# Feed-forward operands moved to starts of their own within 256 bytes, stage by stage

## The chip, the core and the metric

The kernel runs on one core of a Trainium2 chip. The metric is the time of one execution on the device in microseconds (us). Three runs of the kernel before gave 983.25, 983.36 and 985.91; the median is 983.36 us.

The engines are named as in the profile: PE is the matrix engine (PEld its weight loads), DVE the vector engine, ACT the scalar engine, POOL the general one, SP the queue that issues nearly all transfers. SBUF is the on-chip memory of 128 partitions; a "place" below is the byte at which a tile starts in every partition, taken modulo 256. PSUM is the memory that PE writes its sums to.

## The reference

One batch of 256 tokens with 1024 features goes through two layers in float32. What matters here is the feed-forward block, which stands four times in the program, before and after the mixer of each layer:

```python
def swiglu(x, w_gate, w_up, w_down):
    return (jax.nn.silu(x @ w_gate) * (x @ w_up)) @ w_down
...
h = h + 0.5 * swiglu(rms_norm(h, ffn1_norm_g[layer]), ffn1_w_gate[layer],
                     ffn1_w_up[layer], ffn1_w_down[layer])
```

`w_gate` and `w_up` are 1024 x 2816, `w_down` is 2816 x 1024. Between the blocks stand a convolution mixer with memory attention (layer 0), a shared key and value projection, and a block attention mixer with memory attention (layer 1), each with an output projection.

## The kernel before, in words

Activations lie transposed: features over partitions, the 256 tokens along the free dimension. The kernel wants float32 accuracy from products in the faster float32r type, so every operand is split in two: a high part `h` (the value rounded to float32r) and a low part `l` (the rest). A product is made of three of the four partial products, `h*h`, `h*l` and `l*h`.

**Operands.** A streamed operand of a feed-forward stage is one tile `y[P, k, 2, 256]` (or `hs[P, 22, 2, 256]` for the hidden values), in which for each of the `k` blocks of 128 features the high and low parts stand side by side. Weights come from memory in chunks of 2048 columns (`raw`, 1 MB, three buffers, one transfer each on SP's queue). `half_hi` takes half a chunk: ACT copies it into `wh` (line 185: the rounding is the high part) and DVE subtracts `wh` from `raw` into `wl` (line 189). `wh` and `wl` have four buffers of 1024 columns each, that is eight weight tiles of 128 x 128.

**Passes.** One weight load and the stream behind it is called a pass here. For a pair of sums in one PSUM bank, `mm_run` makes from a half chunk eight passes with `wh`, over 512 columns (`y` high and low), and eight passes with `wl`, over 256 columns (`y` high alone). All of them go through line 152. `next_turn` flips which kind goes first, so that two runs of the same kind stand next to each other: `wl` x8, `wh` x8, `wh` x8, `wl` x8 and so on. The last of the eight output tiles of a down projection goes through `mm3` instead, three passes of 256 columns per weight tile.

**Stages.** `ffn` is called four times, with the names a, b, c and d. Each call is two stages: gate and up (22 steps of a gate group and an up group, tiles such as `bg`, `bu`), and down (eight output tiles of 22 weight tiles each, such as `bo`). That makes eight stages with eight streamed operands: `y0`, `ahs`, `oay`, `bhs`, `by1`, `chs`, `oby`, `dhs`. Per call there are 176 wide passes and 176 narrow ones for gate, as many for up, and for down 154 wide and 220 narrow (176 with `wl`, 44 with `wh` in the last output tile). Over the program that is 2024 wide and 2288 narrow passes.

**Order.** A tile framework orders the instructions of each engine from the program's dependencies with its own timing model; tile pools set where each tile lies. The pools are laid one behind another in SBUF: `yp` (streamed operands), `op` (`wh`), `hp` (hidden values), `sp`, `lp` (`wl`), `cp`, `wp` (`raw`), `tp`, `ps` in PSUM. The pool `sp` holds a single small tile `mhalf` of `STEP` = 16 values, 64 bytes, ahead of `lp`. In the built program every streamed operand and every `wh` starts at place 128, and every `wl` at place 192. The same buffers serve the mixers' projections (`ca`, `cg`, `mq`, `bq`, `kv`, `mkv`, `oao`, `obo`). In some of these (`kv`, `bq`, `mq`, `mkv`) the activations are the loaded operand and the weights are streamed.

Of the kernel before, what the change touches and what calls it, by code (L numbers as in the profile page):

```python
# [9 lines left out]
F32 = mybir.dt.float32  # L10
F32R = mybir.dt.float32r
# [6 lines left out]
P = 128  # L18
DM = 1024
KD = DM // P  # L20
SEQ = 256
NT = SEQ // P
DFF = 2816
KF = DFF // P
# [14 lines left out]
HC = 1024  # L39
# [11 lines left out]
MEM_AT = 9  # L51
FIRST_CAT = 3
TURN_AT = 2
STEP = 16
Q_AT = 6
CNR_AT = 4

# [27 lines left out]
def tile_kernel(ctx: ExitStack, tc: tile.TileContext, w, xT, memT, pos, vec, hg, const, out):  # L85
    nc = tc.nc
    yp = ctx.enter_context(tc.tile_pool(name="yp", bufs=2))
    op = ctx.enter_context(tc.tile_pool(name="op", bufs=4))
    hp_ = ctx.enter_context(tc.tile_pool(name="hp", bufs=1))
    sp = ctx.enter_context(tc.tile_pool(name="sp", bufs=1))  # L90
    lp = ctx.enter_context(tc.tile_pool(name="lp", bufs=4))
    cp = ctx.enter_context(tc.tile_pool(name="cp", bufs=1))
    wp = ctx.enter_context(tc.tile_pool(name="wp", bufs=3))
    tp = ctx.enter_context(tc.tile_pool(name="tp", bufs=2))
# [30 lines left out]
    nc.vector.memset(onel, 1.0 / PW)  # L125
    onem = cp.tile([P, P], F32, name="onem")
    nc.vector.memset(onem, 1.0 / PW)
    mhalf = sp.tile([P, STEP], F32, name="mhalf")
    nc.vector.memset(mhalf, -0.5)


    state = {"flip": False, "chunk": 0, "half": 0, "raw": None, "order": "", "last": {}}

    def behind(i, other):
        tc.add_manual_dep(i.ins, other.ins.name,
# [37 lines left out]
    def half_hi():  # L173
        n, h = state["chunk"], state["half"]
        if h == 0:
            state["raw"] = load_chunk(n)
        raw = state["raw"][:, h * HC:(h + 1) * HC]
        wh = op.tile([P, HC], F32R, name=f"wh{n}_{h}", tag="wh", bufs=4)
        wl = lp.tile([P, HC], F32R, name=f"wl{n}_{h}", tag="wl", bufs=4)
        state["chunk"], state["half"] = (n, 1) if h == 0 else (n + 1, 0)  # L180
        q = HC // 2 if n < 2 else HC
        parts = [slice(c, c + q) for c in range(0, HC, q)]

        def hi(s):
            state["act"] = nc.scalar.activation(wh[:, s], raw[:, s], AF.Copy)  # L185
            return state["act"]

        def lo(s):
            state["dve"] = nc.vector.tensor_tensor(wl[:, s], raw[:, s], wh[:, s].bitcast(F32), op=ALU.subtract)  # L189
            return state["dve"]  # L190
        return wh, wl, parts, hi, lo
# [8 lines left out]
    def tiles_of(n_half):  # L200
        for n in range(n_half):
            wh, wl = half_chunk()
            for i in range(8):
                yield wh[:, i * P:(i + 1) * P], wl[:, i * P:(i + 1) * P]
# [47 lines left out]
        return ps.tile([P, 512], F32, name=name, tag=tag, bufs=bufs)  # L252


    def y_tiles(name):
        return yp.tile([P, KD, 2, SEQ], F32R, name=name, tag="y")

    def y_both(name):
        whole = yp.tile([P, KD, 2, SEQ], F32, name=name + "w", tag="y")
        return y_tiles(name), whole[:, :, 0]  # L260

    def scaled_split(y, src, k, g, on_dve=False):
# [62 lines left out]
    def new_acc(name):  # L325
        return tp.tile([P, SEQ], F32, name=name, tag="acc")

    def ffn(name, y, acc, nexts, store=False, both=False, hook=None, after=None, hook_down=None):

        hs = hp_.tile([P, KF, 2, SEQ], F32R, name=name + "hs", tag="hs")  # L330
        rb, first = None, acc is None
        for j in range(KF):
            if hook and j > 1:
                with tc.issue_after(state["act"].ins), tc.issue_after(state["dve"].ins), \
                        tc.issue_after(state["sync"].ins):
                    hook(j)
            if first and j == 0:

                four = [psum(f"{name}{'gu'[i % 2]}{i // 2}") for i in range(4)]
                it = tiles_of(4)  # L340
                for k in range(KD):
                    wts = [next(it) for _ in four]
                    for o, wt in zip(four, wts):
                        mm_passes(mm_run([(o, wt, k)], y)[:1], k == 0, False)
                    for o, wt in zip(four, wts):
                        mm_passes(mm_run([(o, wt, k)], y)[1:], False, k == KD - 1)
                acc = new_acc(name + "acc0")
                nc.scalar.dma_start(cst, const)

                sq = cp.tile([P, KD, SEQ], F32, name="sq0", tag="kv")  # L350
                for k in range(KD):
                    nc.scalar.activation(sq[:, k], x[:, k], AF.Square)
                n = KD
                while n > 1:
                    n //= 2
                    add = nc.vector.tensor_tensor(acc if n == 1 else sq[:, :n].rearrange("p k s -> p (k s)"),
                                                  sq[:, :n].rearrange("p k s -> p (k s)"),
                                                  sq[:, n:2 * n].rearrange("p k s -> p (k s)"), op=ALU.add)
                    if n == KD // 2:
                        behind(add, state["dve"])  # L360
            if first and j < 2:
                pg, pu = four[2 * j:2 * j + 2]
            else:

                at = ("sc", 2) if first and j == 2 else ()
                pg, pu = psum(f"{name}g{j}", *at), psum(f"{name}u{j}", *at)
                if j == 0:

                    wts = [list(tiles_of(1)) for _ in range(2)]
                    for ks in (range(KD - 1), (KD - 1,)):  # L370
                        runs = [mm_run([(o, wt[k], k) for k in ks], y, i == 1)
                                for i, (o, wt) in enumerate(zip((pg, pu), wts))]
                        for run in runs:
                            mm_passes(run, ks[0] == 0, ks[0] > 0)
                else:
                    mm_group2(pg, y)
                    mm_group2(pu, y)
            if rb is None:
                _, rb = norm_stats(name + "n", acc)
            g = both_halves(f"{name}gs{j}", pg, "g")  # L380
            nc.vector.tensor_tensor(g, g, rb, op=ALU.mult)
            s = tp.tile([P, SEQ], F32, name=f"{name}s{j}", tag="s")
            state["func"] = nc.scalar.activation(s, g, AF.Silu)
            h = both_halves(f"{name}h{j}", pu, "h")
            nc.vector.tensor_tensor(h, h, s, op=ALU.mult)
            nc.scalar.activation(hs[:, j, 0], h, AF.Copy)
            nc.vector.tensor_tensor(hs[:, j, 1], h, hs[:, j, 0].bitcast(F32), op=ALU.subtract)
        if after:
            tables(after)
        ys = [(y_both if both else y_tiles)(f"{name}y{i}") for i in range(len(nexts))]  # L390
        acc = new_acc(name + "acc")
        it = tiles_of(KD * KF // 8)
        for m in range(KD):
            po = psum(f"{name}o{m}")
            if hook_down:
                with tc.issue_after(state["act"].ins):
                    hook_down(m)

            both_sums = m < KD - 1
            if both_sums:  # L400
                lead = -m * KF % 8
                cuts = [0] * (lead > 0) + list(range(lead, KF, 8)) + [KF]
                for a, b in zip(cuts, cuts[1:]):
                    jobs = [(po, next(it), k) for k in range(a, b)]
                    mm_passes(mm_run(jobs, hs, next_turn()), a == 0, b == KF)
            else:
                for k in range(KF):
                    mm3(po[:, :SEQ], next(it), hs, k, k == 0, k == KF - 1)
            if both_sums:
                d = both_halves(f"{name}d{m}", po, "g")  # L410
                nc.vector.scalar_tensor_tensor(d, d, 0.5, rb, op0=ALU.mult, op1=ALU.mult)
            else:
                d = tp.tile([P, SEQ], F32, name=f"{name}d{m}", tag="g")
                nc.vector.scalar_tensor_tensor(d, po[:, :SEQ], 0.5, rb, op0=ALU.mult, op1=ALU.mult)
            nc.vector.tensor_tensor(x[:, m], d, x[:, m], op=ALU.add)
            if store:
                nc.sync.dma_start(out[m], x[:, m])
                continue
            last = both and m == KD - 1
            if last:  # L420
                square_sum(f"{name}q{m}", acc, x[:, m], False, nc.vector)
            for yy, g in zip(ys, nexts):
                scaled_split(yy, x[:, m], m, g, last)
            if not last:
                square_sum(f"{name}q{m}", acc, x[:, m], m == 0)
        return ys, acc
# [264 lines left out]
    y = y_tiles("y0")  # L691
# [75 lines left out]

    (y,), acc = ffn("a", y, None, (V_MIX,), both=True, hook=prepare, after=AF.Sigmoid, hook_down=diagonals)

    hc = hp_.tile([P, KF * 2 * SEQ], F32, name="hc", tag="hs")  # L770
    hp = hc[:, :CC * (PAD + SEQ)].rearrange("p (c s) -> p c s", c=CC)
    whole = hc[:, CC * (PAD + SEQ):CC * (PAD + SEQ) + 2 * SEQ].rearrange("p (i s) -> p i s", i=2)
    cv = hc[:, KF * SEQ:KF * SEQ + CC * SEQ].rearrange("p (c s) -> p c s", c=CC)
# [106 lines left out]
    last = psum("cvp2")  # L880
# [308 lines left out]
```

## Time and profile before

| what | value |
|---|---|
| median of the runs | 983.36 us |
| the profiled execution's own time | 984.4 us |
| its span, from the first to the last instruction | 982.6 us |
| granted PE clock, mean | 0.998 |
| PE, PEld busy | 969.8 us, 847.4 us |
| DVE, ACT, POOL busy | 743.2 us, 601.9 us, 125.6 us |
| transfers | 173.47 MB, mean 177 GB/s |

The profiled execution has 1.8 us outside its span, and its time is 1.0 us above the median of the runs. [...] What a pass costs is the distance from its start to the start of the next, and this is what the prediction reads: from the starts in the timeline, or from a piece of the chain of waits, where so many passes in a row took so long together.

### The profile page before, as it was taken

How to read it: one execution, taken by the hardware profiler on the slowest of the kernel's cores; microseconds unless marked ns; L12 is line 12 of the kernel's file. 1: busy time of each engine (PE TensorE's matmuls, PEld its weight loads, DVE VectorE, ACT ScalarE, POOL GpSimd, SP SyncE). 2: the span in 40 equal slices, each digit the busy share in tenths (PEclk: the TensorE clock that was granted, in tenths of full speed). 3: DMA queues.
4: the chain of work that ended last, by engine and by line, in shares of the span. 5: the costliest groups of instructions: out<-in, count | busy, mean ns of one | idle time of the engine just before them, and what ended most of it. 6: DMA issues, size and time to landing. Idle time of an engine off the chain costs nothing.

```text
span 982.6 us, 15395 instructions
## 1 busy us (share of the span) xinstructions
PE 969.8 (99%) x5788; PEld 847.4 (86%) x5788; DVE 743.2 (76%) x1329; ACT 601.9 (61%) x1154; POOL 125.6 (13%) x144
## 2 busy tenths in 40 slices
PE   8999999999999999999999999999998999999998
PEld 6888888898779888888988888888995898888887
DVE  7988776679967887777766777767688588888663
ACT  6676577757576665655646665655556656565542
POOL 0011000138713000000123000000152030000000
PEclk9999999999999999999999999999999999999999
DMA  8655555534325555555545555555452056554560
GB/s 313 246 190 179 204 177 201 188 124 134 125 91 200 205 191 185 201 178 186 193 174 186 183 187 180 206 179 206 174 174 83 9 198 223 176 205 177 185 222 22
DMA packets 26427, 173.47 MB, mean 177 GB/s; under 512 B 3184, under 2 KB 4848, under 8 KB 6000
## 3 DMA queue, kind: packets, MB, share of 16 engines
q1 hardware_dynamic: 26064, 172.31, 49.9%
q8 instruction: 45, 0.74, 0.3%
q14 instruction: 30, 0.25, 0.1%
q10 hardware_dynamic: 288, 0.17, 0.1%
HBM read 171.43 MB, written 1.05 MB: 176 GB/s over the span
## 4 chain that ended last, share of the span: by engine, by line
PE 91%; DVE 3%; ACT 2%; POOL 2%; DMA 1%; issue 1%; POOLq 0%; ACTq 0%; DVEq 0%
PE cg L152 7%; PE dg L152 6%; PE bg L152 6%; PE do L152 6%; PE bo L152 6%; PE co L152 6%; PE ao L152 6%; PE bu L152 6%; PE du L152 6%; PE cu L152 6%; PE au L152 6%; PE ag L152 6%; PE kv L152 3%; PE oao L152 2%; PE obo L152 2%; PE mkv L152 2%
## 5 line engine op out<-in xcount | busy, mean ns | idle before, releaser
L189 DVE TENSOR_TENSOR wl<-raw,wh 128x1024 fp32r<-128x1024 f32 (+1 forms) x310 | 377.0, 1220 | 99.8 <-ACT wh L185 95.5
L185 ACT ACTIVATE wh<-raw 128x1024 fp32r<-128x1024 f32 (+1 forms) x310 | 324.2, 1050 | 119.7 <-PE do L152 20.4
L152 PE MATMUL ag<-y,wh 128*128 128x512 f32 x176 | 46.8, 394 | 1.5 <-ACT wh L185 1.5
L152 PE MATMUL au<-y,wh 128*128 128x512 f32 x176 | 46.9, 394 | 0.0
L152 PE MATMUL do<-dhs,wh 128*128 128x512 f32 (+1 forms) x198 | 45.4, 367 | 0.0
L152 PE MATMUL bo<-bhs,wh 128*128 128x512 f32 (+1 forms) x198 | 45.4, 367 | 0.0
L152 PE MATMUL co<-chs,wh 128*128 128x512 f32 (+1 forms) x198 | 45.3, 367 | 0.0
L152 PE MATMUL ao<-ahs,wh 128*128 128x512 f32 (+1 forms) x198 | 45.1, 366 | 0.0
L152 PE MATMUL bg<-oay,wh 128*128 128x512 f32 x176 | 45.0, 393 | 0.0
L152 PE MATMUL dg<-oby,wh 128*128 128x512 f32 x176 | 44.6, 393 | 0.0
L152 PE MATMUL cu<-by,wh 128*128 128x512 f32 x176 | 44.4, 393 | 0.0
L152 PE MATMUL cg<-by,wh 128*128 128x512 f32 x176 | 43.9, 391 | 0.4 <-DVE cgs L242 0.4
L152 PE MATMUL du<-oby,wh 128*128 128x512 f32 x176 | 44.0, 389 | 0.0
L152 PE MATMUL bu<-oay,wh 128*128 128x512 f32 x176 | 44.0, 389 | 0.0
L850 POOL TENSOR_TENSOR hc<-hc,cq 128x256 f32<-128x256 f32 x58 | 42.3, 730 | 13.2 <-ACT cq L849 9.4
L858 DVE SCALAR_TENSOR_TENSOR cvp<-hc,vt,cvp 128x256 f32<-128x256 f32 x88 | 40.6, 484 | 1.5
L152 PEld LDWEIGHTS ag<-y,wh 128*128 128x128 f32 x176 | 33.1, 189 | 8.7 <-ACT wh L185 1.9
L152 PEld LDWEIGHTS ao<-ahs,wh 128*128 128x128 f32 x198 | 34.8, 188 | 5.3
L152 PEld LDWEIGHTS cg<-by,wh 128*128 128x128 f32 x176 | 32.9, 188 | 7.5 <-DVE cgs L242 0.8
L152 PEld LDWEIGHTS co<-chs,wh 128*128 128x128 f32 x198 | 34.8, 188 | 5.3
L152 PEld LDWEIGHTS do<-dhs,wh 128*128 128x128 f32 x198 | 34.8, 188 | 5.3
L152 PEld LDWEIGHTS bo<-bhs,wh 128*128 128x128 f32 x198 | 34.8, 188 | 5.3
(996 smaller groups left out, 2136.8 us busy)
## 6 DMA issues: line engine op xcount, KB each, us to landing
raw<-in_w SPq DMA_DIRECT2D x158, 1024.0 KB, 4.8
raw<-in_w SPq DMA_DIRECT2D x5, 512.0 KB, 9.2
mT<-in_memT SPq DMA_DIRECT2D x1, 1024.0 KB, 8.1
out<-x SPq DMA_DIRECT2D x8, 128.0 KB, 1.7
raw<-in_w SPq DMA_DIRECT2D x2, 256.0 KB, 3.9
x<-in_xT SPq DMA_DIRECT2D x1, 512.0 KB, 7.7
x<-in_xT SPq DMA_DIRECT2D x2, 128.0 KB, 3.3
x<-in_xT SPq DMA_DIRECT2D x1, 256.0 KB, 5.6
```

The source lines that it names most:

```text
L152: return in_order("P", nc.tensor.matmul(*a, **k))
L185: state["act"] = nc.scalar.activation(wh[:, s], raw[:, s], AF.Copy)
L189: state["dve"] = nc.vector.tensor_tensor(wl[:, s], raw[:, s], wh[:, s].bitcast(F32), op=ALU.subtract)
L850: state["pool"] = nc.gpsimd.tensor_tensor(cv[:, c], cv[:, c], q, op=ALU.add)
L858: nc.vector.scalar_tensor_tensor(cv[:, c] if end else o, win(c, i), tap[c][i], o, op0=ALU.mult, op1=ALU.add)
```

## The change

The change is in where tiles lie. `wh`, `wl`, the streamed operands, the hidden tile and `hc` (which uses the hidden tile's buffer in the mixer) each get 64 values (256 bytes) more than they need, and `shifted` cuts out the part that starts at the wanted place. `HOMES` lists for each of the eight stages the places of the streamed operand, of `wh` and of `wl`; everywhere else all three stand at 128 (`NO_HOME`). `state["homes"]` is switched at the start of a call of `ffn`, ahead of its down projection, and behind its last output tile. The pools `sp` and `lp` are gone: `wl` moves to the pool of `wh`, `mhalf` to that of the constants. The room comes from the scratch that the framework keeps at the bottom of SBUF for transfers described in software, 8 KB instead of 16 KB.

```diff
@@ -51,7 +51,11 @@
-STEP = 16
+HOME_AT = 128
+SLACK = 64
+HOMES = {"y0": (0, 0, 64), "ahs": (0, 128, 128), "oay": (0, 192, 192), "bhs": (0, 64, 0),
+         "by1": (128, 0, 0), "chs": (128, 192, 128), "oby": (64, 0, 128), "dhs": (192, 192, 0)}
+NO_HOME = (128, 128, 128)
@@ -87,8 +91,6 @@
-    sp = ctx.enter_context(tc.tile_pool(name="sp", bufs=1))
-    lp = ctx.enter_context(tc.tile_pool(name="lp", bufs=4))
@@ -125,11 +127,11 @@
-    mhalf = sp.tile([P, STEP], F32, name="mhalf")
+    mhalf = cp.tile([P, 16], F32, name="mhalf")
@@ -175,8 +177,8 @@
-        wh = op.tile([P, HC], F32R, name=f"wh{n}_{h}", tag="wh", bufs=4)
-        wl = lp.tile([P, HC], F32R, name=f"wl{n}_{h}", tag="wl", bufs=4)
+        wh = shifted(op.tile([P, HC + SLACK], F32R, name=f"wh{n}_{h}", tag="wh", bufs=4), state["homes"][1])
+        wl = shifted(op.tile([P, HC + SLACK], F32R, name=f"wl{n}_{h}", tag="wl", bufs=4), state["homes"][2])
@@ -252,11 +254,18 @@
+    def shifted(t, home):
+        a = (home - HOME_AT) % 256 // 4
+        return t[:, a:a + t.shape[1] - SLACK]
+
+    def at_home(t, name):
+        return shifted(t, HOMES.get(name, NO_HOME)[0]).rearrange("p (k a s) -> p k a s", a=2, s=SEQ)
+
     def y_tiles(name):
-        return yp.tile([P, KD, 2, SEQ], F32R, name=name, tag="y")
+        return at_home(yp.tile([P, KD * 2 * SEQ + SLACK], F32R, name=name, tag="y"), name)
@@ -327,8 +336,9 @@
-        hs = hp_.tile([P, KF, 2, SEQ], F32R, name=name + "hs", tag="hs")
+        hs = at_home(hp_.tile([P, KF * 2 * SEQ + SLACK], F32R, name=name + "hs", tag="hs"), name + "hs")
         rb, first = None, acc is None
+        state["homes"] = HOMES[{"a": "y0", "b": "oay", "c": "by1", "d": "oby"}[name]]
@@ -389,6 +399,7 @@
         acc = new_acc(name + "acc")
+        state["homes"] = HOMES[name + "hs"]
@@ -413,6 +424,8 @@
+            if m == KD - 1:
+                state["homes"] = NO_HOME
@@ -767,7 +780,7 @@
-    hc = hp_.tile([P, KF * 2 * SEQ], F32, name="hc", tag="hs")
+    hc = hp_.tile([P, KF * 2 * SEQ + SLACK], F32, name="hc", tag="hs")
@@ -1177,7 +1190,7 @@
-    nc = bacc.Bacc("TRN2", target_bir_lowering=False, num_devices=1)
+    nc = bacc.Bacc("TRN2", target_bir_lowering=False, num_devices=1, dynamic_dma_scratch_size=8192)
```

In the built program each engine issues the same instructions in the same order as before, on all five engines. What differs is addresses. One wait differs too: in the convolution, DVE's wait for POOL's clearing of `hc` stands one instruction earlier, at the product `hc<-cas,cs` (line 830) instead of the tap behind it (line 854).

The places of the streamed operand, `wh` and `wl` by stage, from the addresses of the built programs; "distance" is the loaded operand's place less the streamed one's, modulo 256, for `wh` and for `wl`:

| stage | before | distance | after | distance |
|---|---|---|---|---|
| a, gate and up (`y0`) | 128, 128, 192 | 0, 64 | 0, 0, 64 | 0, 64 |
| a, down (`ahs`) | 128, 128, 192 | 0, 64 | 0, 128, 128 | 128, 128 |
| b, gate and up (`oay`) | 128, 128, 192 | 0, 64 | 0, 192, 192 | 192, 192 |
| b, down (`bhs`) | 128, 128, 192 | 0, 64 | 0, 64, 0 | 64, 0 |
| c, gate and up (`by1`) | 128, 128, 192 | 0, 64 | 128, 0, 0 | 128, 128 |
| c, down (`chs`) | 128, 128, 192 | 0, 64 | 128, 192, 128 | 64, 0 |
| d, gate and up (`oby`) | 128, 128, 192 | 0, 64 | 64, 0, 128 | 192, 64 |
| d, down (`dhs`) | 128, 128, 192 | 0, 64 | 192, 192, 0 | 0, 64 |
| mixers' projections | 128, 128, 192 | 0, 64 | 128, 128, 128 | 0, 0 |

The memory projection `mkv` that stands inside the first gate and up stage takes that stage's weights (0 and 64) with its own activations at 128. The `raw` buffers, into which the weights are transferred, stay at place 96. The constants and `x` move by 64 bytes modulo 256.

More of the change, by code (lines that the diff above doesn't have):

```diff
@@ L127, in tile_kernel @@
     nc.vector.memset(onem, 1.0 / PW)
-    mhalf = sp.tile([P, STEP], F32, name="mhalf")
+    mhalf = cp.tile([P, 16], F32, name="mhalf")
     nc.vector.memset(mhalf, -0.5)
-    state = {"flip": False, "chunk": 0, "half": 0, "raw": None, "order": "", "last": {}}
+    state = {"flip": False, "chunk": 0, "half": 0, "raw": None, "order": "", "last": {}, "homes": NO_HOME}
     def behind(i, other):
@@ L252, in psum @@
         return ps.tile([P, 512], F32, name=name, tag=tag, bufs=bufs)
+    def shifted(t, home):
[3 more added lines that the diff above has]
+        return shifted(t, HOMES.get(name, NO_HOME)[0]).rearrange("p (k a s) -> p k a s", a=2, s=SEQ)
     def y_tiles(name):
-        return yp.tile([P, KD, 2, SEQ], F32R, name=name, tag="y")
+        return at_home(yp.tile([P, KD * 2 * SEQ + SLACK], F32R, name=name, tag="y"), name)
     def y_both(name):
-        whole = yp.tile([P, KD, 2, SEQ], F32, name=name + "w", tag="y")
+        whole = at_home(yp.tile([P, KD * 2 * SEQ + SLACK], F32, name=name + "w", tag="y"), name)
         return y_tiles(name), whole[:, :, 0]
```

## The prediction

> **What bounds the kernel now.** I read the page first (the span, the busy shares, the chain of work that ended last), then what PE waits for, then PE's timeline.
>
> ```profile
> span 982.6 us, 15395 instructions
> PE 969.8 (99%) x5788; PEld 847.4 (86%) x5788; DVE 743.2 (76%) x1329; ACT 601.9 (61%) x1154; POOL 125.6 (13%) x144
> PEclk9999999999999999999999999999999999999999
> ...
> PE 91%; DVE 3%; ACT 2%; POOL 2%; DMA 1%; issue 1%; POOLq 0%; ACTq 0%; DVEq 0%
> ...
> PE ab2s L152 <- ACT q1T L456: 1.8, 1, 1.8
> PE ag L152 <- ACT wh L185: 1.5, 2, 1.3
> ```
>
> PE is 91% of the chain at full granted clock. The last two rows are the largest of nine in the list of PE's waits; none is over 1.8 us. So the end moves only when PE's own passes take more or less time. An edit that moves no instruction can do that in one way: by changing what a pass costs. The groups by shape give the counts, for one gate and one down stage:
>
> ```profile
> L152 PE MATMUL ag<-y,wh 128*128 128x512 f32 x176 | 46.8, 394 | 1.5 <-ACT wh L185 1.5
> L152 PE MATMUL ag<-y,wl 128*128 128x256 f32 x176 | 26.2, 281 | 0.0
> ...
> L152 PE MATMUL ao<-ahs,wh 128*128 128x512 f32 x154 | 37.3, 391 | 0.0
> L152 PE MATMUL ao<-ahs,wl 128*128 128x256 f32 x176 | 26.5, 281 | 0.0
> L152 PE MATMUL ao<-ahs,wh 128*128 128x256 f32 x44 | 7.8, 281 | 0.0
> ```
>
> The 394 and 281 ns overlap each other, so the cost of a pass comes from starts. One period of stage b in PE's timeline (start, length, then the run; x8 is eight passes):
>
> ```profile
> 360.50 1.10 PE L152 MATMUL bu<-oay,wl 128*128 128x256 f32 x8
> 361.44 1.11 PE L152 MATMUL bg<-oay,wl 128*128 128x256 f32 x8
> 362.39 2.00 PE L152 MATMUL bg<-oay,wh 128*128 128x512 f32 x8
> 364.23 1.97 PE L152 MATMUL bu<-oay,wh 128*128 128x512 f32 x8
> 366.04 1.10 PE L152 MATMUL bu<-oay,wl 128*128 128x256 f32 x8
> ```
>
> Sixteen narrow passes take 362.39 - 360.50 = 1.89 us, **118.1 ns each**. The eight wide ones behind the turn from `wl` to `wh` take 1.84 us, **230 ns each**, and the next eight 1.81 us, **226 ns each**. Same tiles, same shape, same place: a run of wide passes starts slow behind a turn and settles at 226. The chain of waits, in which a piece is so many passes in a row, shows what else the same two shapes cost:
>
> ```profile
> 143.55 61.14 PE ao L152 x374
> ...
> 216.68 3.45 PE ca L152 x16
> ...
> 299.47 10.25 PE oao L152 x87
> ...
> 494.82 7.66 PE kv L152 x33
> ...
> 735.10 4.80 PE bq L152 x40
> ```
>
> A whole down stage: 220 narrow passes at 118.1 are 26.0 us, which leaves 35.1 us for 154 wide ones, **228.3 each**. `oao`, narrow, where the loaded operand changes between place 128 and 192 from pass to pass: 117.8 each. `kv`, wide, and `bq`, narrow, where it is the streamed operand that changes between 128 and 192: **232.1** and **120.0**. The feed-forward passes together are 2288 x 118.1 + 1408 x 228 + 616 x 228.3 ns = 270 + 321 + 141 = 732 us, 74% of the span. One nanosecond on every one of them is 4.3 us.
>
> There is one more pace in the trace, early in stage b, where the framework mixes short runs:
>
> ```profile
> 312.41 0.86 PE L152 MATMUL bu<-oay,wh 128*128 128x512 f32 x3
> 313.11 0.96 PE L152 MATMUL bg<-oay,wl 128*128 128x256 f32 x7
> 313.90 0.63 PE L152 MATMUL bg<-oay,wh 128*128 128x512 f32 x2
> ```
>
> Seven narrow passes with `wl` in 0.79 us: **112.9 ns each**, at the same places as the 118.1. They stand behind a wide run of only three passes, which had not settled. So a narrow run has at least two paces, and the one it falls into depends on how it is entered. That is what makes places count: a different distance between `wh` and `wl` changes how the loads stand to the stream at each turn.
>
> **The change part by part.** It adds no instruction, no transfer and no byte of traffic, and moves none past another.
>
> *The six stages whose distances change* (`ahs`, `oay`, `bhs`, `by1`, `chs`, `oby`) hold 3 x 352 = 1056 gate and up passes of each width and 3 x 154 = 462 wide and 3 x 220 = 660 narrow down passes. Bounds from the rows: a narrow pass lies between 112.9 and 120.0, now 118.1; a wide run between 226 throughout and 232.1, now 228 on average. At the good end: 1716 x 5.2 ns = 8.9 us, half of 1056 wide passes x 4 ns = 2.1 us, and 462 x 2.3 ns = 1.1 us, together 12.1 us saved. At the bad end: 1716 x 1.9 ns = 3.3 us, 1056 x 4.1 ns = 4.3 us, 462 x 3.8 ns = 1.8 us, together 9.4 us lost. No row has these distances in this order of passes. I take the good side, because the narrow passes stand nearer to their slow bound than to their fast one and the narrow term is the largest, and half of it, because six different settings won't all enter the fast pace: **6.0 us saved**.
>
> *The two stages that keep their distances* (`y0` and `dhs`, 0 and 64): nothing, if only the distance counts. `oao` supports it in part: jumps of 64 in the loaded operand left 117.8. If the place itself counts, all eight stages join: at the good end 2288 x 5.2 + 704 x 4 + 616 x 2.3 ns = 16.1 us saved, at the bad end 2288 x 1.9 + 1408 x 4.1 + 616 x 3.8 ns = 12.4 us lost. I take zero.
>
> *The mixers*: `wl` goes from 192 to 128. In `kv` and `bq` the streamed operand then stops jumping. At the steady paces this is worth 144 x 6.1 ns + 144 x 1.9 ns = 1.2 us; at the other end, nothing. Between them I take the middle, **0.6 us saved**.
>
> *ACT and DVE* write `wh` and `wl` to other places. In stage b:
>
> ```profile
> core 0: us, PE busy (x) PEld busy (x) DVE busy (x) ACT busy (x) POOL busy (x), PEclk, DMA share, GB/s
> ...
> 330.00:430.00 100.00, 100.00 (x579) 88.31 (x578) 81.27 (x132) 61.40 (x109) 0.00 (x0) 1.00 0.54 190
> ```
>
> DVE has 18.7 us in 100 free and ACT 38.6, so even a subtraction slower by a tenth stays behind PE. PE faster by 2% takes 2 of these 18.7. Without that cover the price would be DVE's pace, a fifth of which is slack. I cost it at nothing.
>
> *The scratch of 8 KB, and the earlier wait on POOL.*
>
> ```profile
> q1 hardware_dynamic: 26064, 172.31, 49.9%
> ...
> q10 hardware_dynamic: 288, 0.17, 0.1%
> ...
> raw<-in_w SPq DMA_DIRECT2D x158, 1024.0 KB, 4.8
> ...
> L779 POOL MEMSET hc<- x1: 112/112/112, 204.9 to 204.9; 128x15 f32 x1
> ...
> L830 DVE TENSOR_TENSOR hc<-cas,cs x5: 418/726/915, 212.4 to 239.5; 128x256 f32<-128x256 f32 x5
> ```
>
> The data queues are of the hardware kind and no transfer is issued by POOL, so the halved scratch serves nothing here. If transfers slowed nonetheless, a chunk lands in 4.8 us and is used up in one period of 5.54 us (366.04 - 360.50) with three buffers: landing could take twice as long before PE noticed. POOL's clearing of `hc` ends at 205.0, and the instruction that now waits for it starts at 212.4. Both nothing. If that cover were gone, the wait would hold the taps queued behind it on DVE, and with them the convolution.
>
> **Sum.** 6.0 + 0.6 = 6.6 us off the profiled execution's 984.4 gives 977.8. That execution is 1.0 us above the median of the runs (983.36), so on the median it is 976.8. I say **977 us**. A change within 0.3% (2.95 us) can't be told from none with this measurement.
>
> **The rivals.**
>
> *Nothing depends on place* (983). The 118.1 of the `wl` runs at distance 64 and the 117.8 of `oao`, where distance 0 and 64 alternate, are the same. If paces come from the entry alone and every entry settles as before, only the mixers' share is left, 0 to 1.2 us. Against it: `kv` and `bq` do cost more than the same shapes elsewhere. [...]
>
> *The runs don't settle* (993, the slower side). In `kv` successive passes meet at changing distances and never come down to 226. If a new distance, such as 192 for `oby`'s wide passes and 64 for its narrow ones, leaves loads and streams in each other's way throughout, wide passes go to 232.1 and narrow ones to 120.0: 9.4 us lost in the six stages, 992.8 on the median, 995.8 with all eight. It decides as soon as a third of the six stages lie there and the others stay. For it: 226 is the best steady wide pace seen, so wide passes can hardly improve beyond the turns and can easily get worse. Against it: within a run of eight the distance is constant, as it isn't in `kv`.
>
> *A much deeper gain* (935). The plain float32 passes of `ca` take 3.45 us / 16 = 215.6 ns for 256 columns. If float32r could reach half of that, 107.8 narrow and 215.6 wide, the feed-forward passes would save 2288 x 10.3 + 2024 x 12.4 ns = 48.7 us. No row of float32r comes near; it bounds the matter from below. [...]
>
> **How the numbers follow.** The forecast, a gain from better entries in part of the stages: 0.50, with 970 to 980 as its own range. Nothing depends on place: 0.22. The runs don't settle: 0.22. A deeper gain, even a third of the way (967 and below): 0.06. The range of 967 to 988 reaches from all eight stages at their good end (983.4 - 16.1 - 0.6 = 966.7) over no change to half of the bad end of six (988.1). Below it lies about 0.06, above it 0.12 of the 0.22. Faster by over 0.3%: 0.50 + 0.06 = 0.56; within: 0.22; slower: 0.22.
>
> **What would show it right or wrong.** Narrow runs at 113 in at least three of the six stages, in the same timeline rows, with `y0` and `dhs` at 118; down stages of 60 us in place of 61.14; `kv` near 226 a pass and `bq` near 118. Rows in stage b equal to those quoted would say that nothing depends on place. Wide runs at 232 would show the third case. It is wrong in its grounds if `y0` or `dhs` change pace as much as the others (the place, not the distance), or if PE's list of waits has a new row of several us, which would mean that DVE, ACT or a transfer paid for the move.

## The result: 0.5% slower

The changed kernel takes 989.41 us (median of three runs, 988.93 to 989.48) against 983.36; the ratio is 1.0052, with a 95% interval of 1.0027 to 1.0077. The forecast was 977 with a range of 967 to 988.

The page of the changed kernel, its engines and the chain by engine, and the largest of PE's waits:

```profile
span 987.7 us, 15393 instructions
PE 976.3 (99%) x5788; PEld 849.1 (86%) x5788; DVE 744.2 (75%) x1329; ACT 600.9 (61%) x1154; POOL 125.9 (13%) x144
...
PE 92%; ACT 2%; DVE 2%; POOL 2%; DMA 1%; issue 1%; SPq 0%; POOLq 0%; ACTq 0%; DVEq 0%
...
PE ab2s L154 <- ACT q1T L469: 1.5, 1, 1.5
```

PE is busy 6.5 us longer with the same 5788 passes, and waits for nobody more than before. No other engine pays for the move. So the loss is in what a pass costs, and the down stages show it at once. The chain of waits of the kernel before (in all of these, x374 is one whole down stage):

```profile
296.42 2.83 PE oao L152 x24
...
433.62 61.19 PE bo L152 x374
...
653.32 61.16 PE co L152 x374
...
917.87 61.21 PE do L152 x374
```

And of the changed kernel:

```profile
142.22 61.95 PE ao L154 x374
...
296.05 2.87 PE oao L154 x24
...
433.06 61.93 PE bo L154 x374
494.99 7.51 PE kv L154 x33
...
654.56 61.99 PE co L154 x374
...
922.93 61.20 PE do L154 x374
```

The down stages of a, b and c, whose distances changed, are 0.74 to 0.83 us longer (`ao` was 61.14). `do`, which moved from place 128 to 192 and kept its distances, is where it was. `kv` went from 232.1 to 227.6 ns a pass, `oao` from 117.9 to 119.6. In gate and up, PE's timeline of the changed kernel in stage b (distances 192, 192):

```profile
380.52 2.00 PE L154 MATMUL bu<-oay,wh 128*128 128x512 f32 x8
382.36 1.07 PE L154 MATMUL bu<-oay,wl 128*128 128x256 f32 x8
383.26 1.07 PE L154 MATMUL bg<-oay,wl 128*128 128x256 f32 x8
384.17 1.99 PE L154 MATMUL bg<-oay,wh 128*128 128x512 f32 x8
386.00 1.99 PE L154 MATMUL bu<-oay,wh 128*128 128x512 f32 x8
387.83 1.10 PE L154 MATMUL bu<-oay,wl 128*128 128x256 f32 x8
388.77 1.10 PE L154 MATMUL bg<-oay,wl 128*128 128x256 f32 x8
389.71 1.55 PE L154 MATMUL bg<-oay,wh 128*128 128x512 f32 x6
```

and in stage c (distances 128, 128):

```profile
607.55 2.03 PE L154 MATMUL cu<-by,wh 128*128 128x512 f32 x8
609.41 2.03 PE L154 MATMUL cg<-by,wh 128*128 128x512 f32 x8
611.28 1.12 PE L154 MATMUL cg<-by,wl 128*128 128x256 f32 x8
612.24 1.11 PE L154 MATMUL cu<-by,wl 128*128 128x256 f32 x8
613.18 2.03 PE L154 MATMUL cu<-by,wh 128*128 128x512 f32 x8
```

Stage b alternates between two paces of the narrow runs: 384.17 - 382.36 = 1.81 us for sixteen, **113 ns each**, then 389.71 - 387.83 = 1.88 us, 117.5. That is the fast pace of the forecast, in every second period. Its wide runs no longer settle at 226; they stay at 229. Stage c has neither: sixteen wide passes in 611.28 - 607.55 = 3.73 us, **233 each**, and narrow ones at 119.

By stage, from the first pass of one stage to the first pass of the next in the two traces (to the last pass for the down stages), in us:

| stage | distances after | before | after | difference |
|---|---|---|---|---|
| a, down | 128, 128 | 61.02 | 61.83 | +0.81 |
| b, gate and up | 192, 192 | 123.91 | 123.49 | -0.42 |
| b, down | 64, 0 | 61.07 | 61.81 | +0.74 |
| c, gate and up | 128, 128 | 123.85 | 125.54 | +1.69 |
| c, down | 64, 0 | 61.04 | 61.86 | +0.82 |
| d, gate and up | 192, 64 | 122.62 | 124.18 | +1.56 |
| **the six together** | | | | **+5.20** |
| d, down | 0, 64 (kept) | 61.08 | 61.07 | 0.0 |
| `kv` | 0, 0 | 34.77 | 34.14 | -0.6 |
| other mixers | 0, 0 | 186.03 | 187.85 | +1.8 |
| a, gate and up | 0, 64 (kept) | 137.19 | 135.86 | -1.3 |

The sum is the 5.1 us by which the spans differ. The last row is not the change's: this stage begins while the first weights arrive (PE waits 1.5 us there for ACT's `wh` in the trace of the kernel before, 0.3 in that of the changed kernel), and in three other runs at these distances it took 136.1 to 137.3. Nor are about 1.4 us of "other mixers": with the same places there, in the run of the mixers alone below, they took 186.48. The windows view of the block attention, of the kernel before and then of the changed kernel, has the granted clock behind the busy times:

```profile
core 0: us, PE busy (x) PEld busy (x) DVE busy (x) ACT busy (x) POOL busy (x), PEclk, DMA share, GB/s
742.00:768.00 26.00, 21.96 (x160) 14.04 (x160) 21.74 (x85) 19.12 (x76) 1.64 (x3) 0.93 0.12 41
```

```profile
742.00:768.00 26.00, 22.49 (x154) 13.91 (x154) 21.80 (x82) 17.52 (x65) 3.30 (x5) 0.87 0.13 43
```

In this stage, where PE has pauses, the clock falls to half for 3.4 us in the trace of the kernel before, for 6.8 in that of the changed kernel, and not at all in some others (1.00 in these 26 us with the feed-forward stages alone, below). Executions of one and the same kernel spread with it by up to 4 us: those of the kernel before took 985.55 to 986.36 at a granted clock of 0.996 or less, and 982.24 to 984.48 above it. So time differences of about 1 us are read from stages below, not from totals.

### The profile page after: what moved, and what is told of

Read it like the earlier page. It is cut to its first block, busy times and chain, and to the rows that moved or that the text cites. A ratio compares the mean times of both kernels' runs of the same rounds, so it can differ in the third digit from the quotient of the medians.

```text
span 987.7 us, 15393 instructions
## 1 busy us (share of the span) xinstructions
PE 976.3 (99%) x5788; PEld 849.1 (86%) x5788; DVE 744.2 (75%) x1329; ACT 600.9 (61%) x1154; POOL 125.9 (13%) x144
## 4 chain that ended last, share of the span: by engine, by line
PE 92%; ACT 2%; DVE 2%; POOL 2%; DMA 1%; issue 1%; SPq 0%; POOLq 0%; ACTq 0%; DVEq 0%
PE cg L154 7%; PE co L154 6%; PE ao L154 6%; PE dg L154 6%; PE bo L154 6%; PE du L154 6%; PE do L154 6%; PE bu L154 6%; PE bg L154 6%; PE cu L154 6%; PE au L154 6%; PE ag L154 6%; PE kv L154 3%; PE oao L154 2%; PE obo L154 2%; PE mkv L154 2%
## 5 line engine op out<-in xcount | busy, mean ns | idle before, releaser
L154 PEld LDWEIGHTS du<-oby,wh 128*128 128x128 f32 x176 | 33.0, 189 | 7.5
```

Of the source, the lines that this page charges most:

```text
L154: return in_order("P", nc.tensor.matmul(*a, **k))
```

## The experiments

The theory after the result: **the distance between loaded and streamed operand, modulo 256, sets a pass's pace**, the place doesn't, and the table picks distances that are worse for wide passes. Its rivals: the place itself, the slack or the halved scratch cost the time; the mixers carry it; the pace comes from the entry into a run rather than from the distance.

**Distances kept, everything else changed.**

```diff
-HOMES = {"y0": (0, 0, 64), "ahs": (0, 128, 128), "oay": (0, 192, 192), "bhs": (0, 64, 0),
-         "by1": (128, 0, 0), "chs": (128, 192, 128), "oby": (64, 0, 128), "dhs": (192, 192, 0)}
-NO_HOME = (128, 128, 128)
+HOMES = {"y0": (0, 0, 64), "ahs": (0, 0, 64), "oay": (0, 0, 64), "bhs": (0, 0, 64),
+         "by1": (128, 128, 192), "chs": (128, 128, 192), "oby": (64, 64, 128), "dhs": (192, 192, 0)}
+NO_HOME = (128, 128, 192)
```

> Keeps the change's layout, slack, 8 KB scratch and its places of the streamed operand (0, 0, 0, 0, 128, 128, 64, 192 by stage), but puts every wh at distance 0 and every wl at distance 64 from it, in the mixers too. If only the distance between loaded and streamed operand counts: the time of before, 983 to 984, and every down stage near 61.05 us. If the place itself, the slack or the scratch cost the 6 us: 987 to 990, with stage b's down at 61.8 again.

Measured: 983.43 against 983.54 us, ratio 1.0001 (0.9991 to 1.0010). Its chain of waits:

```profile
142.45 61.14 PE ao L154 x374
...
432.44 61.19 PE bo L154 x374
...
652.12 61.16 PE co L154 x374
```

These are the three numbers of the kernel before, to the hundredth, with the streams at 0, 0 and 128. So the place, the slack, the pools and the 8 KB of scratch cost nothing that shows within 0.1%. What counts is the distance.

**Maps of the distances.** Four kernels with all streams at place 128 and a pair of distances of its own in each stage. Only the table differs: a row gives the place of the streamed operand, of `wh` and of `wl`, so the distances are the second and third less the first.

```diff
 # first map
+HOMES = {"y0": (128, 64, 192), "ahs": (128, 128, 128), "oay": (128, 128, 128), "bhs": (128, 128, 0),
+         "by1": (128, 128, 0), "chs": (128, 128, 64), "oby": (128, 128, 64), "dhs": (128, 64, 64)}
+NO_HOME = (128, 128, 0)
```

> Streamed operands all at 128. Gate and up distances (wh, wl): a (192, 64), b (0, 0), c (0, 128), d (0, 192); down: a (0, 0), b (0, 128), c (0, 192), d (192, 192); mixers (0, 128). Distance theory, each kind of pass by its own distance: wide 228 a pass on average where wh is at 0, 233 at 192; narrow 118, 119.3 and 117 for wl at 0 (or 64), 128, 192. So against before stage a gate and up +1.6 us, b 0, c +0.4, d -0.3; down a 0, b +0.3, c -0.2, d +0.5. Entry theory, the pair counts: d's down goes as b's gate and up went with (192, 192), wide 229, narrow 117, -0.1 us. If the place itself counts, a's gate and up needn't repeat the 233 that d's had at the same distances with the stream at 64.

```diff
 # second map
+HOMES = {"y0": (128, 192, 128), "ahs": (128, 64, 192), "oay": (128, 192, 192), "bhs": (128, 64, 0),
+         "by1": (128, 192, 0), "chs": (128, 64, 128), "oby": (128, 192, 64), "dhs": (128, 192, 192)}
+NO_HOME = (128, 128, 64)
```

> Streamed operands all at 128. Gate and up distances: a (64, 0), b (64, 64), c (64, 128), d (64, 192); down: a (192, 64), b (192, 128), c (192, 0), d (64, 64); mixers (0, 64), as before. Distance theory: wide 233.5 in all gate and up stages, each 1.7 to 2.3 us longer than before, down stages 0.6 to 1.0 us longer, mixers as before. Entry theory: some pair falls into a better pace, wide at 229 or below, as (192, 192) did.

```diff
 # third map
+HOMES = {"y0": (128, 0, 128), "ahs": (128, 0, 128), "oay": (128, 64, 64), "bhs": (128, 0, 192),
+         "by1": (128, 0, 192), "chs": (128, 0, 64), "oby": (128, 0, 64), "dhs": (128, 192, 0)}
+NO_HOME = (128, 192, 192)
```

> Streamed operands all at 128. Gate and up distances: a (128, 0), b (192, 192), c (128, 64), d (128, 192); down: a (128, 0), b (128, 64), c (128, 192), d (64, 128); mixers (64, 64). Distance theory: b's gate and up repeats the change's -0.4 us against before though its stream is at 128 and not at 0 (place theory: it needn't); wide at 128 costs 232.8, so c and d +1.2 to +1.9 us, downs +0.5 to +0.9. Entry theory: pairs of 128 scatter around that by more than 2 ns a pass.

```diff
 # fourth map
+HOMES = {"y0": (128, 64, 128), "ahs": (128, 128, 160), "oay": (128, 128, 160), "bhs": (128, 128, 224),
+         "by1": (128, 128, 224), "chs": (128, 128, 96), "oby": (128, 128, 96), "dhs": (128, 192, 64)}
+NO_HOME = (128, 192, 192)
```

> Streamed operands at 128. Gate and up: a (192, 0), b (0, 32), c (0, 96), d (0, 224); down: a (0, 32), b (0, 96), c (0, 224), d (64, 192); mixers (64, 64). Wide passes with wh at 0 should be at 228 to 229 whatever wl's distance (a pass's own distance counts first), so b, c, d gate and up within 0.7 us of before; if wl's distance of an odd multiple of 32 spoils the turns as it did with (224, 192), wide 230 or more. A narrow pace of 113 together with wide 228 in one of them would make a pair better than (192, 192).

The executions, one of each, took 987.28, 986.67, 988.14 and 985.58 us, the first three beside 983.5 for the kernel before and the last beside 983.2. The down stages, from the traces of these four, of the change and of the kernel before: wide and narrow ns per pass (the mean from start to start, passes that something interrupted left out), and in brackets the stage against before in us:

| `wh` at | `wl` at 0 | `wl` at 64 | `wl` at 128 | `wl` at 192 |
|---|---|---|---|---|
| 0 | 229.0, 119.6 (+0.42) | 228.8, 117.8 (before) | 228.9, 119.6 (+0.38) | 230.9, 117.4 (+0.24) |
| 64 | 233.5, 118.2 (+0.78) | **232.9, 113.8 (-0.28)** | 232.7, 118.5 (+0.72) | 232.7, 116.4 (+0.23) |
| 128 | 232.0, 119.0 (+0.77) | 232.1, 116.8 (+0.25) | 232.8, 118.7 (+0.81) | 232.8, 116.6 (+0.35) |
| 192 | 229.3, 118.8 (+0.28) | 230.8, 116.7 (+0.08) | 230.6, 118.1 (+0.32) | 229.4, 117.3 (-0.05) |

A wide pass goes first by its own distance: 229 to 231 at 0 and at 192, 232 to 233.5 at 64 and 128. A narrow one likewise: slow at 0 and 128, quicker at 64 and 192. But not only: narrow passes at 64 take 117.8 beside wide ones at 0 and 113.8 beside wide ones at 64. Gate and up says the same in fewer words: (192, 192) is 0.4 us better than before at place 0 and at place 128 alike (123.49 and 123.47 us), (64, 64) is 0.2 us worse, (0, 0), (0, 128), (0, 192) and (128, 64) are 0.5 to 0.6 us worse, (64, 128), (64, 192), (128, 128), (128, 192) and (192, 64) 1.3 to 1.7 us worse. The expectations that let each kind go by its own distance alone failed in most stages. In the first map five of seven missed, (192, 192) in d's down among them (0.5 us longer expected, -0.05 measured). In the second all four down stages missed (0.6 to 1.0 us longer expected, -0.3 to +0.3 measured), in the third three of seven stages: the pair counts. Of the last map, the narrow pace of 113 beside a wide one of 228 was found nowhere. (0, 32) in b's gate and up missed what was expected, with wide passes at 230.3 and the stage 0.8 us longer; (0, 224) in d's gate and up came nearest, with 229.0 and 116.6, 0.3 us better than before.

**A finer grain.** The same kind of table with odd multiples of 32 bytes, and then with 16 bytes off the good pairs.

```diff
 # odd multiples of 32
+HOMES = {"y0": (128, 96, 96), "ahs": (128, 160, 160), "oay": (128, 32, 32), "bhs": (128, 224, 224),
+         "by1": (128, 64, 96), "chs": (128, 192, 224), "oby": (128, 96, 64), "dhs": (128, 224, 192)}
+NO_HOME = (128, 160, 160)
```

> Distances that are odd multiples of 32 bytes: gate and up a (224, 224), b (160, 160), c (192, 224), d (224, 192); down a (32, 32), b (96, 96), c (64, 96), d (96, 64); mixers (32, 32). If only the 64-byte part of a distance counts (banks of 64 bytes): 224 acts as 192, 160 as 128, 32 as 0, 96 as 64, so wide 229.4 in a, c, d and 232.8 in b, and c's and d's down near (64, 64) with 233 and 114. If a finer grain counts: values between or outside of these, and perhaps a pair under 228 wide and 116 narrow.

```diff
 # 16 off
+HOMES = {"y0": (128, 128, 144), "ahs": (128, 208, 208), "oay": (128, 80, 80), "bhs": (128, 176, 176),
+         "by1": (128, 48, 48), "chs": (128, 192, 208), "oby": (128, 128, 208), "dhs": (128, 208, 192)}
+NO_HOME = (128, 192, 192)
```

> Distances 16 bytes off the good pairs, streamed operands at 128: gate and up a (0, 16), b (208, 208), c (176, 176), d (0, 80); down a (80, 80), b (48, 48), c (64, 80), d (80, 64); mixers (64, 64). If the grain is 32 bytes (16 bytes off changes nothing): b's gate and up 123.5 as with (192, 192), a's and c's down 60.8 as with (64, 64). If it is finer: these go 0.5 us and more above, as the distances of 32 did (61.6 to 61.9 in down).

Measured: 992.57 and 987.44 us, one execution of each. (32, 32), (96, 96), (64, 96) and (96, 64) made down stages of 61.6 to 61.9 us, and (160, 160) a gate and up stage 2.4 us longer than before, with wide passes at 233 and narrow ones at 120. (224, 192) in d's gate and up had wide passes at 232.6, where 229.4 was expected if only the 64-byte part counts; the banks of 64 bytes behind that are the author's supposition, and no run shows them. At 16 bytes off, (80, 80) and (64, 80) gave 61.7 and 61.8 where (64, 64) gives 60.8; (80, 64) came nearer, with 61.2. PE's timeline of that kernel in stage b, with (208, 208):

```profile
362.31 2.03 PE L154 MATMUL bg<-oay,wh 128*128 128x512 f32 x8
364.17 2.03 PE L154 MATMUL bu<-oay,wh 128*128 128x512 f32 x8
366.04 1.09 PE L154 MATMUL bu<-oay,wl 128*128 128x256 f32 x8
```

Wide passes at 3.73 us / 16 = 233, where (192, 192) has 229. So 16 bytes count, and a grain of 64 or 32 bytes doesn't explain the paces.

**The two halves of the change.** The mixers alone, and the feed-forward stages alone.

```diff
 # the mixers alone
+HOMES = {"y0": (128, 128, 192), "ahs": (128, 128, 192), "oay": (128, 128, 192), "bhs": (128, 128, 192),
+         "by1": (128, 128, 192), "chs": (128, 128, 192), "oby": (128, 128, 192), "dhs": (128, 128, 192)}
 NO_HOME = (128, 128, 128)
```

> The change's places in the mixers alone (all three at 128, distances 0 and 0); every feed-forward stage keeps distances 0 and 64 as before. From the paces of the change: kv 4.4 ns a pass faster (0.6 us), but the narrow projections at 120 in place of 118 (oao, obo, bq, mq, ca: some 0.9 us slower). Feed-forward theory of the 6 us: 983 to 984.5, within 1 us of before. If the mixers carried a third of the loss: 985.5 or more.

```diff
 # the feed-forward stages alone: the change's HOMES
-NO_HOME = (128, 128, 128)
+NO_HOME = (128, 128, 192)
```

> The change's table for the eight feed-forward stages, but the mixers keep distances 0 and 64 as before. The change's stages were 5.2 us longer than before in the six whose distances differ, and the mixers alone cost 1.0 us. If the two add up: 988 to 989, stage by stage as in the change. If the loss needs both (a pace carried from a mixer into the next stage): 986 or less.

The mixers alone: 984.48 against 983.49, ratio 1.0015 (1.0006 to 1.0024), 1.0 us, within what was expected of the feed-forward theory. Part of this 1.0 us goes with the clock: four of the eleven executions had a granted clock of 0.994 to 0.996 and took 985.8 to 986.1, and none of the kernel before had less than 0.997. In the trace, where the granted clock is 0.998 as before, `kv` is 0.6 us shorter and the other mixers 0.4 us longer, together 0.2 us less. The feed-forward stages alone: 990.81 against 983.18, ratio 1.0067 (1.0046 to 1.0089), above the 988 to 989 expected. Three of its five executions had a granted clock of 0.995 and took 990.8 to 991.5; the two at 0.998 and 1.0 took 988.0 and 987.0. Its stages are the change's own:

```profile
142.46 61.95 PE ao L154 x374
...
432.87 61.93 PE bo L154 x374
...
654.97 61.99 PE co L154 x374
```

and in gate and up 123.47, 125.51 and 124.16 us for b, c and d. So the loss is the feed-forward stages', and they lose the same with or without the mixers' part. The rest of this run's total goes with the granted clock: the kernel before took 982.4 to 983.8 at 0.998 and above, some 5 us less than the two executions here, and 985.6 and 985.9 at 0.996 and 0.994. No trace shows where the three longer executions lost their time.

**What a turn costs.** The kernel before, with the flip taken away, so that every wide run stands behind a narrow one:

```diff
     def next_turn():
-        state["flip"] = not state["flip"]
-        return not state["flip"]
+        return False
```

> The kernel before at its own places, but every group of passes runs wh first and wl second (next_turn always says no), so a wide run always stands behind a narrow one: one turn per group in place of one per two. Turn theory: every wide run of eight then starts slow, 230 a pass and not 228, 704 x 4 ns in gate and up and about 616 x 1.7 ns in down, 3 to 4 us longer, near 987. If the slow wide passes came from the subtraction that DVE runs at that time and not from the turn: within 1 us of before.

Measured: 987.00 against 983.49, ratio 1.0038 (1.0024 to 1.0052), 3.5 us. Its timeline in stage b:

```profile
360.40 2.00 PE L152 MATMUL bu<-oay,wh 128*128 128x512 f32 x8
362.24 1.11 PE L152 MATMUL bu<-oay,wl 128*128 128x256 f32 x8
363.18 2.00 PE L152 MATMUL bg<-oay,wh 128*128 128x512 f32 x8
365.02 1.11 PE L152 MATMUL bg<-oay,wl 128*128 128x256 f32 x8
```

Every wide run now takes 362.24 - 360.40 = 1.84 us, 230 ns a pass, as only the first after a turn did. The slow start belongs to the turn. The stage lengths grew by less than the total: 0.15 and 0.37 us in b's and d's gate and up and 0.17 to 0.21 in each of the four downs, about 1.3 us; c's gate and up was 0.33 shorter, where the kernel before had one interrupted pass of 0.7 us. Most of the rest stands in a's gate and up: it took 139.2 us against 137.2, with two pauses of PE, 0.5 and 1.2 us long, behind DVE's `ags` and `ah` (line 241), which the kernel before doesn't have. So the slow start is shown by its pace, and the 3.5 us are not its price alone.

**Is it the distance or the entry?** A pair with the narrow pace of 113 in a's down, and then the same kernel with (128, 0) there, which leaves the pace of 118 to 119. The convolution's passes behind it, `ca` and `cg`, stand at the same places in both.

```diff
-HOMES = {"y0": (128, 64, 64), "ahs": (128, 192, 192), "oay": (128, 64, 64), "bhs": (128, 192, 192),
+HOMES = {"y0": (128, 64, 64), "ahs": (128, 0, 128), "oay": (128, 64, 64), "bhs": (128, 192, 192),
```

> As the run with the best pairs, except the down projection of stage a: (128, 0) in place of (64, 64). The convolution's float32r passes (ca, first two groups) that follow have the same places in both. Entry theory: they take up the pace that the down stage before them leaves, 117.7 as after (128, 0) in the map, in place of 113.4, and keep it; a's down itself 61.8 in place of 60.8. If the distance alone sets the pace: ca stays at 113.4.

The chain of waits of the first, the run with the best pairs:

```profile
142.25 60.89 PE ao L154 x374
209.26 2.75 PE ca L154 x24
...
294.33 2.74 PE oao L154 x24
```

and of the second:

```profile
141.74 61.91 PE ao L154 x374
209.96 2.83 PE ca L154 x24
...
295.31 2.83 PE oao L154 x24
```

24 passes of `ca` in 2.75 and in 2.83 us, 114.6 and 117.9 ns each, at the same distances (64, 64); `oao`, which comes 80 us and many other passes later, the same. From start to start the settled paces are 113.3 and 117.7. So at one pair of distances there are two paces, and what ran before decides between them (the second kernel has one execution). But a stage doesn't simply take over the pace of the one before it. The kernel with 16 bytes off has (64, 64) in the mixers too, behind a down stage of a with narrow passes at 118.7:

```profile
142.76 61.85 PE ao L154 x374
...
210.73 2.75 PE ca L154 x24
...
295.93 2.83 PE oao L154 x24
```

There `ca` has the fast pace behind a slow stage, and `oao` the slow one. What decides at the entry is not shown. In the feed-forward stages what ran before made no such difference: (64, 64) gave narrow passes at 113.7 to 114.0 in all eight down stages, of three kernels, that had it.

**The best pairs together.** (192, 192) in gate and up, (64, 64) in down and in the mixers:

```diff
+HOMES = {"y0": (128, 64, 64), "ahs": (128, 192, 192), "oay": (128, 64, 64), "bhs": (128, 192, 192),
+         "by1": (128, 64, 64), "chs": (128, 192, 192), "oby": (128, 64, 64), "dhs": (128, 192, 192)}
+NO_HOME = (128, 192, 192)
```

> Streamed operands at 128; (192, 192) in all four gate and up stages, (64, 64) in all four down stages, (64, 64) in the mixers: the best pairs of the maps so far. If a stage's time is its own pair's and nothing else, the stages add up: 4 x 0.42 us in gate and up, 4 x 0.27 us in down, some 0.8 us in the mixers, 3.5 us less than before, about 980. If the maps' small gains were scatter, or a pair's pace depends on the stage it follows: within 1 us of before.

Measured: **978.48** against 983.49 us, ratio **0.9952** (0.9940 to 0.9965), 5.0 us less than the kernel before and about 11 less than the change. Gate and up of b, c and d took 123.51, 123.42 and 122.12 us (0.40, 0.43 and 0.50 less), the four downs 60.77 to 60.85 (0.19 to 0.30 less). These add to 2.4 us, near the sum of their pairs. In the mixers 0.8 us was expected and the trace has 2.2 us less: `ca`, `mq` and `oao` run at 114, where the same places in the third map ran at 117.7.

## Why the prediction was wrong

*What bounds the kernel* was right: PE's passes, and nothing else, moved the time. *The turn* was right in its pace: 230 behind one, 226 when settled at distance 0, and without the flip 230 everywhere. *The rival that place itself counts* was rightly set to zero: `dhs` at 192 and `do` at 61.20, and the run with the distances kept at 1.0001.

*The six stages* is the step that failed: "I take the good side", and half of its 12.1 us, **6.0 us saved**, where the stages lost **5.2 us**. Of its two terms the narrow one was let decide because 118.1 lies nearer to 120.0 than to 112.9. The runs showed that most distances do little for the narrow passes (116.4 to 119.6 in fifteen of the sixteen pairs of the down stages, 113.8 only at (64, 64)), while `wh` at 64 or 128 costs the wide ones about 4 ns. The table puts `wh` at 64 or 128 in four of the six stages and at 192 in the others, in d's gate and up with `wl` at 64, which costs the same there: wide passes at 233 in five stages, 462 x 4.5 + 704 x 4.3 ns = 5.1 us. One stage, b's gate and up, gained: its narrow runs had the pace of 113 in every second period, and it came out 0.4 us shorter. The sign asked for was this pace in at least three stages. The wide bound was also set too low, 232.1 from `kv` against 232.7 to 233.7 measured.

The mechanism behind that step was only partly right. The prediction let places act through the entry into a run at each turn, which its author inferred from two narrow paces, 112.9 and 118.1, at the same places. In the stages that lost, the cost is not at the turns: at (192, 64) and (128, 128) wide passes stay at about 233 from the first pass of a run to the last.

The argument that should have weighed more stood under the rival: 226 was the best wide pace seen, so wide passes could get worse at nearly any other distance and better at none. The kernel before already stood at a `wh` distance at which a wide run settles, at 226; in the change's trace none did at the others, with 229 at (192, 192) and about 233 at 64, at 128 and at (192, 64). *The runs don't settle* named what came for the wide passes and bounded its price (9.4 us at most, 992.8; 5.2 us measured in the stages); its other half, narrow passes at 120.0, didn't come (117.7 to 118.7 in the five stages). What was said against it, that the distance within a run is constant, was no obstacle.

*The mixers*: the term for `kv` was right, 232.1 to 227.6, 0.6 us where up to 0.9 was said. The term for `bq` rested on a misreading. In the kernel before, `mq`, whose streamed operand jumps in the same way, and a piece of `bq` itself already ran at 118:

```profile
714.48 5.18 PE mq L152 x44
...
728.56 3.89 PE bq L152 x33
```

That is 117.7 and 117.9 ns a pass, so the 120.0 was not the price of the jumps. With the jumps gone `bq` is at 119.7, and the narrow projections settle at about 119.8 at distance 0 throughout, where the jumps between 0 and 64 had kept them at 118. By the trace of the mixers alone their sum is 0.2 us less, not 0.6.

*ACT and DVE, scratch, POOL's wait* at nothing: right, by the unchanged waits and the run with the distances kept. *Nothing depends on place* is refuted for places relative to each other: the same stage takes 60.8 to 61.9 us by distances alone. Why some distances cost more than others isn't shown by any run. *A much deeper gain* has no support: its 107.8 and 215.6 were an estimate, half and all of what the plain float32 passes of `ca` take, and over some thirty pairs no feed-forward stage had wide passes under 228 or narrow ones under 113 on average.

## What to carry to other kernels

In this kernel, where PE is the bound (99% of the span busy) and its passes run back to back, the start of a loaded and of a streamed float32r operand relative to each other, down to 16 bytes, was worth 1% of the time (978.48 against 989.41 us), and their absolute place nothing that could be measured (a ratio of 1.0001 with the distances kept). Read the pace of each run of passes from start to start before changing it, per width: a shape that already runs at the best pace seen has more to lose than to gain, and here it was the wide passes, which settle at 226 ns at distance 0, that carried 63% of the feed-forward time. A table of places has to be measured as a whole: the feed-forward stages kept the pace of their pair (narrow passes at 113.7 to 114.0 in all eight down stages at (64, 64)), but the mixers' narrow passes had one of two paces, 113.3 or 117.7, at the same pair.

## What the runs showed of the hardware that wasn't expected

Narrow passes at one and the same pair of distances, (64, 64) in the mixers, run at 113.3 or at 117.7 ns and can stay there for over a hundred passes (`oao`). Which of the two depends on what ran before, and not simply on the pace of the stage before. Distances that are off by 16 bytes can undo the better pace: a's down took 61.7 us at (80, 80) and 60.8 at (64, 64). And plain constancy is no cure: narrow passes at distance 0 throughout settle at 119.8, slower than the 118 that they run at when every third pass jumps by 64 bytes.
